# Where the modulation weights land while two projections run: slots of their own in the second branch projection and the output projection

## The chip, the cores and the metric

The kernel runs on one core of a Trainium2 chip. The core has five engines that run side by side, each through its own list of instructions in order: TensorE (PE in the profile; its weight loads stand apart as PEld) multiplies matrices, VectorE (DVE) and ScalarE (ACT) work on tiles element by element, GpSimd (POOL) and SyncE (SP) here mostly issue transfers. They meet only through semaphores. The metric is the device time in microseconds (us), the median over runs; lower is better.

## The reference

One decoder layer over 512 tokens of width 2048, in float32. A conditioning vector c is turned into six vectors of 2048 numbers ("ada", the modulation), and they shift, scale and gate the two halves of the layer:

```python
mod = (c_act @ w_ada[l] + b_ada[l])[:, None, :]
sh_a, sc_a, gt_a, sh_f, sc_f, gt_f = jnp.split(mod, N_ADA, axis=-1)
h = rms_norm(x, g_attn[l]) * (1.0 + sc_a) + sh_a
# inside parallel_mixers: sparse attention o_a, dense latent attention o_b
merged = jax.nn.sigmoid(gate_a) * (o_a @ w_pa) + jax.nn.sigmoid(gate_b) * (o_b @ w_pb)
return merged @ w_o
# and in the layer
x = x + gt_a * y
h = rms_norm(x, g_ffn[l]) * (1.0 + sc_f) + sh_f
x = x + gt_f * conv_ffn(h, w_up[l], w_conv[l], b_conv[l], w_down[l])
```

`w_ada` is 2048 x 12288. Its first third (shift and scale of the first half) is needed at the very beginning. The other two thirds are sixteen blocks of 2048 x 512, 67 MB, of which nothing is needed before the output projection ends: `gt_a` multiplies its result, `sc_f` and `sh_f` come next, `gt_f` comes last of all.

## The kernel before, in words

**Matrices.** Each float32 factor is cut into a high part that the fast matmul format holds exactly and a low part, the rest. A product is three matmuls (`mm3`, lines 117 to 119): high by high, high by low, low by high. A step of a projection, in `lin_fm` and `lin_tm` alike, takes two blocks of 128 rows by 512 columns of weights, which is one 512 KB load, one ScalarE copy that makes the high part (line 105), one VectorE subtraction that makes the low part (line 106, the tile is called `wlo`; "the correction" below), and 24 matmuls of 512 columns. The two stages called `seven` (gates of the mixer, from `w_gs`, and the feed-forward's `w_ups`) save one product in eight by adding and subtracting weight blocks first (VectorE, line 929); their steps have 24 matmuls of 256 columns, with the low parts at line 114.

**Buffers.** Weights land in a ring of five buffers, `raw` (`NR` is 5, `rawq` hands them out in turn). High and low parts have three buffers each (`NH` is 3), so a correction can run at most until three steps have been made ready and not yet multiplied. Everything else lives in 81 slots of 128 x 512 numbers, handed out first in, first out by `get` and given back by `put`.

**The ada stream.** `ada_stream` (line 702) works through the sixteen late blocks in steps, 8 steps to a block, 128 in all. One step loads 256 rows of a block's 512 columns (512 KB) and adds them, times `c_act`, to the block's accumulator `acc` with two VectorE instructions (line 720 for a block's first, line 722 for the others; "the products" below). The load goes either to one buffer of the `raw` ring (one transfer, line 714) or, while `ada_in_slots[0]` is true, to two slots (two transfers of 256 KB, line 710). A finished block waits in `pend` until `flush_cols` (lines 752 to 769) sums it over the partitions with two matmuls.

**Who calls the steps.** `ticker(rate)` returns a function that every step of a stage calls once; it adds `rate` to a credit and runs one ada step for each whole credit. The stages after the first input projection are, in the order of time of the profile before:

- the attention of branch A with some gate columns in between, until about 600 us: 35 ada steps;
- the gate stage, `seven` on `w_gs`, 56 steps, to about 795 us: rate `TS`;
- the first branch projection by `w_pa`, 16 steps, mixed with the attention of branch B, to about 1025 us: rate `TP`;
- the second branch projection by `w_pb`, 16 steps in four column blocks, to about 1127 us: rate `TB`. For each column block `load_gates` brings twelve tiles (projection A's result and both gates) through GpSimd's queue, and `ev_pb` combines them on VectorE (lines 1208, 1216, 1217, and the low part at line 114);
- the output projection by `w_o`, 32 steps in four column blocks, to about 1333 us: rate `TO`. `ev_o` multiplies by the gate and adds x (lines 1249, 1250);
- then the second norm and the feed-forward.

**Order.** The functions are written as plain loops, but the order of each engine's list is made by the framework's scheduler, which runs its own estimate of time. Weight loads and their high and low parts are issued with a raised priority (`PRI`). All weight loads and all ada loads go through SyncE's one queue, in order; a transfer waits there until its buffer is free, and everything behind it waits too.

Of the kernel before, what the change touches and what calls it, by code (L numbers as in the profile page):

```python
# [31 lines left out]
def trunk_layer_kernel(  # L32
# [8 lines left out]
    U1=4,  # L41
    U2=10,
    PLAN="A0 A1|A2 A3|B0 B1 B2 B3|A4 A5 A6 A7|B4 B5 B6 B7|A8 A9 A10 A11|B8 B9 B10 B11|A12 A13 A14 A15 B12 B13 B14 B15",
    TS=0.55,
    TP=1,
    TB=1,
    TO=1,
    HG=2,
    AFT=(-1,),
    PEU=((2, 5, 8, 11, 14),) * 2 + ((),) * 6,  # L50
# [14 lines left out]
    def get(dt=F32):  # L65
        i = free.popleft()
        if cur[i] is None or cur[i].dtype != dt:
            cur[i] = pool.tile([P, T], dt, name=f"slot{i}", tag=f"slot{i}")
        held[id(cur[i])] = i
        return cur[i]  # L70

    def getr():
        return get(F32R)

    def put(*ts):
        for t in ts:
            free.append(held.pop(id(t)))
# [415 lines left out]
    def at_bank():  # L493
        cnt["at"] += 1
        return AT[cnt["at"] % 4]
# [25 lines left out]
    for tb in range(1, 4):  # L521
# [12 lines left out]
        acc = get()  # L534
# [45 lines left out]
    def head_ss(dst, src3, i):  # L580
        n, d = src3.shape[1], src3.shape[2]
        t = sq[i % 2][:, :n * d].rearrange("p (n d) -> p n d", n=n)
        A.activation(t, src3, AF.Square)
        V.tensor_reduce(dst, t, axis=AX.X, op=ALU.add)
# [54 lines left out]
    def attend_free(kinds="pto"):  # L639
        for k in kinds:  # L640
            put(*att[k])
# [52 lines left out]

    ada_blocks = [8, 9, 10, 11, 16, 17, 18, 19, 12, 13, 14, 15, 20, 21, 22, 23]
    gst = [get(), get()]
    ada_acc = [get(), get()]

    ada_in_slots = [False]

    def ada_stream():
        for n, cb in enumerate(ada_blocks):
            assert len(pend) < 2
            acc = ada_acc[n % 2]
            for kp in range(8):
                if ada_in_slots[0]:
                    ts = [get(), get()]
                    for i in range(2):
                        k = kp * 2 + i
                        SP.dma_start(ts[i], w_ada[k * P:(k + 1) * P, cb * 512:(cb + 1) * 512])  # L710
                else:
                    raw = rawq.popleft()
                    t = raw[:, 0:1024].rearrange("p (k n) -> p k n", k=2)
                    SP.dma_start(t, w_ada[kp * 2 * P:(kp + 1) * 2 * P, cb * 512:(cb + 1) * 512]
                                 .rearrange("(k p) n -> p k n", p=P))
                    ts = [t[:, 0], t[:, 1]]
                for i in range(2):
                    k = kp * 2 + i
                    if k == 0:
                        V.tensor_scalar(acc, ts[i], c_act[:, 0:1], None, op0=ALU.mult)  # L720
                    else:
                        V.scalar_tensor_tensor(acc, ts[i], c_act[:, k:k + 1], acc,  # L722
                                               op0=ALU.mult, op1=ALU.add)
                if ada_in_slots[0]:
                    put(*ts)
                else:
                    rawq.append(raw)
                yield None
            pend.append((cb, acc))
            done[0] += 1  # L730

    pend = []
# [6 lines left out]
    def ticker(rate, fb=None):  # L739
        def tick():  # L740
            credit[0] += rate
            while credit[0] >= 1.0:
                credit[0] -= 1.0
                next(stream, None)
                age[0] = age[0] + 1 if pend else 0
                if fb and age[0] > 3:
                    flush_cols(fb())
        return tick
# [109 lines left out]
    def fill(n, ticks=0):  # L858
        for _ in range(n):
            if next(gates, 0) == 0:  # L860
                break
            for _ in range(ticks):
                tick()
# [4 lines left out]
    for hd in range(9):  # L868
# [10 lines left out]
            attend_pv(*prev)  # L879
        fill(1, 2)  # L880
        prev = state
    ada_in_slots[0] = False
    fill(26, 1)
    put(*kaT)
    put(*kva)
# [17 lines left out]
    def operands(act, ts):  # L903
        return (quarter(act, 0, 0), quarter(act, KH, 0), quarter(act, KH, HT)) + tuple(sums(ts, n) for n in range(4))
# [151 lines left out]
    def reload_mq():  # L1056
        for t in h[:KH]:
            put(*t)
        mqT.extend(reload(mq_d))

    ada_in_slots[0] = True
    seven(w_gs, (31 - G0) // 2, operands(h, h_sums), ((MM[0], MM[1]), (MM[2], MM[3])), gate_out,
          tick=ticker(TS, at_bank), near_end=reload_mq)
    ada_in_slots[0] = False
    for t in h[KH:] + [x for ts in h_sums for x in ts]:
        put(*t)
    gst = [get(), get()]
# [5 lines left out]
    def up_pair(hp):  # L1073
        kn = [get() for _ in range(2)]
        vv = [get() for _ in range(2)]
        kr = get()
        kr3 = kr.rearrange("p (t a d) -> p t a d", t=4, a=2)

        def two(ts, tb):
            o = (tb % 2) * 256  # L1080
            return ts[tb // 2][:, o:o + 256].rearrange("p (n d) -> p n d", n=2)

        def ev_up(tb, b, kn=kn, vv=vv, kr3=kr3, two=two):
            b4 = b.rearrange("p (n e d) -> p n e d", n=2, e=2)
            k3 = two(kn, tb)
            A.activation(k3, b4[:, :, 0, :], AF.Copy)
            V.tensor_copy(two(vv, tb), b4[:, :, 1, :])
            ss = sm.tile([P, 2], F32, name="ss2")
            head_ss(ss, k3, tb)
            V.tensor_scalar(ss, ss, ss_kr[:, tb:tb + 1], None, op0=ALU.add)  # L1090
            r = sm.tile([P, 2], F32, name="rs2")
            rsqrt_mean(r, ss, 192, 2)
            V.tensor_tensor(k3, k3, r[:, :, None].to_broadcast([P, 2, P]), ALU.mult)
            for a in range(2):
                V.tensor_scalar(kr3[:, tb, a], krot[:, tb], r[:, a:a + 1], None, op0=ALU.mult)

        lin_tm(w_mkv_up, hp * 512, 512, kvT, 2, MM, ev_up)
        kT = [get(), get()]
        kTr = (getr(), getr())
        for a in range(2):  # L1100
            b = at_bank()
            for tb in range(4):
                PE.transpose(b[:, tb * P:(tb + 1) * P], two(kn, tb)[:, a, :], ident)
            A.activation(kT[a], b, AF.Copy, scale=gkm_col)
        b = at_bank()
        for tb in range(4):
            PE.transpose(b[:, tb * P:(tb + 1) * P], kr[:, tb * P:(tb + 1) * P], ident)
        split(*kTr, b)
        put(*kn)
        put(kr)  # L1110

        qn = [get() for _ in range(2)]
        qr = get()
        qr3 = qr.rearrange("p (t a d) -> p t a d", t=4, a=2)
        nsc_b = sm.tile([P, 4, 2], F32, name="nsc_b", bufs=3)

        def ev_qup(tb, b, qn=qn, qr3=qr3, nsc_b=nsc_b, two=two):
            b3 = b.rearrange("p (n d) -> p n d", n=2)
            q3 = two(qn, tb)
            A.activation(q3, b3[:, :, 0:P], AF.Copy)  # L1120
            V.tensor_copy(qr3[:, tb], b3[:, :, P:192])
            ss = sm.tile([P, 2], F32, name="ss2")
            t = sq[tb % 2][:, :384].rearrange("p (n d) -> p n d", n=2)
            A.activation(t[:, :, 0:P], q3, AF.Square)
            A.activation(t[:, :, P:192], qr3[:, tb], AF.Square)
            V.tensor_reduce(ss, t, axis=AX.X, op=ALU.add)
            r = sm.tile([P, 2], F32, name="rs2")
            rsqrt_mean(r, ss, 192, 2)
            V.tensor_scalar(nsc_b[:, tb], r, -(192 ** -0.5), None, op0=ALU.mult)
            rope(qr3[:, tb], 2, 64, "qm", tb)  # L1130

        lin_tm(w_mq_up, hp * 384, 384, mqT, 4, MM, ev_qup)
        qT = [get(), get()]
        qTr = (getr(), getr())
        for a in range(2):
            b = at_bank()
            for tb in range(4):
                PE.transpose(b[:, tb * P:(tb + 1) * P], two(qn, tb)[:, a, :], ident)
            A.activation(qT[a], b, AF.Copy, scale=gqm_col)
        b = at_bank()  # L1140
        for tb in range(4):
            PE.transpose(b[:, tb * P:(tb + 1) * P], qr[:, tb * P:(tb + 1) * P], ident)
        split(*qTr, b)
        put(*qn)
        put(qr)
        pairs[hp] = (qT, qTr, kT, kTr, vv, nsc_b, two)
# [25 lines left out]
    def pa_block(cb):  # L1172
        flush_cols(MM[3])
        lin_fm(w_pa, cb * 512, oa, 8, MM, ev_store(pa_d, cb * 4), tick=ticker(TP))

    up_pair(0)
    oa = reload(oa_d)
    up_pair(1)
    attend_bufs()
    for hp in range(4):  # L1180
        attend_pair(hp)
        pa_block(hp)
        if hp < 2:
            up_pair(hp + 2)
    attend_free("pt")
    for t in oa:
        put(*t)
    for t in kvT + mqT:
# [35 lines left out]
    for cb in range(4):  # L1224
        bk = half()
        flush_cols(bk[3])
        lin_fm(w_pb, cb * 512, ob, 8, bk, ev_pb(load_gates(cb)), tick=ticker(TB))
    for t in ob:
# [37 lines left out]
    for db in range(4):  # L1266
        bk = half()
        flush_cols(bk[3])
        lin_tm(w_o, db * 512, 512, mg, KD, bk, ev_o(db), tick=ticker(TO))
    while next(stream, 0) is None:  # L1270
# [188 lines left out]
```

## Time and profile before

| | |
|---|---|
| median of 3 runs | 2723.09 us (2720.21 to 2723.1) |
| the profiled execution | 2732.41 us |
| its span on the core | 2730.6 us |
| TensorE busy | 2661.8 us, 97% of the span |
| VectorE busy | 1941.3 us, 71% |
| ScalarE busy | 1153.6 us, 42% |
| bytes moved | 437.25 MB, mean 160 GB/s |
| ada loads in `raw` buffers / in slots | 71 of 512 KB / 242 of 256 KB, of which 128 in the first stage |

Busy time counts a matmul until its modelled end, so TensorE's 97% is not 97% of its peak: where matmuls follow each other at full pace their spacing is what to look at. "Granted clock" (PEclk) is the share of TensorE's clock pulses that were let through. A row of waits names the waiting instruction, then what it waited for, then the total in us, the number of waits and the longest. A row of windows gives, for each engine, the busy us and the number of instructions in brackets, then the clock, the share of time the 16 DMA engines were busy, and GB/s.

### The profile page before, as it was taken

Reading aid. Unit: us, or ns where it says so; the run is one execution under the profiler, and the core shown is the slowest. Engines: PE = TensorE matmul, PEld = TensorE weight load, DVE = VectorE, ACT = ScalarE, POOL = GpSimd, SP = SyncE. Lnnn points to the kernel's source line nnn. Section 1 sums busy time; section 2 is a strip of 40 time slices with the busy share of each in tenths; the row PEclk is TensorE's granted clock in tenths of the full one; section 3 lists DMA queues with packets and bytes.
Section 4 is the critical chain, followed back from the end, with each engine's and each line's share of the span. In section 5 each row is a group of like instructions: output and inputs, shape, how many; then the busy total and the mean of one; then the engine's idle time right before and its main releaser. Section 6 shows DMA issues by size and latency. Waiting matters only on the chain.

```text
span 2730.6 us, 40272 instructions
## 1 busy us (share of the span) xinstructions
PE 2661.8 (97%) x15616; PEld 2303.0 (84%) x15616; DVE 1941.3 (71%) x3059; ACT 1153.6 (42%) x1713; POOL 240.9 (9%) x459
## 2 busy tenths in 40 slices
PE   6999999999999999998999999999999999999999
PEld 5777687778987767776789999999999998888887
DVE  7877966699887666745678888888888873325323
ACT  4333434334344564322445555555555553223221
POOL 1001011110022232100000000000000040000000
PEclk8999999999999999999999999999999999999999
DMA  9943137666684578755423333333333384343232
GB/s 342 341 149 100 34 103 224 199 197 211 212 273 140 175 237 257 252 179 181 138 85 122 126 113 124 117 119 120 116 128 114 119 298 129 98 125 124 93 115 78
DMA packets 197572, 437.25 MB, mean 160 GB/s; under 512 B 19290, under 2 KB 60660, under 8 KB 197380
## 3 DMA queue, kind: packets, MB, share of 16 engines
q1 hardware_dynamic: 165700, 348.59, 39.7%
q0 software_dynamic: 31648, 86.08, 9.6%
q8 instruction: 122, 2.00, 0.3%
q14 instruction: 70, 0.57, 0.1%
q10 hardware_dynamic: 32, 0.01, 0.0%
HBM read 390.56 MB, written 44.04 MB: 159 GB/s over the span
## 4 chain that ended last, share of the span: by engine, by line
PE 75%; issue 10%; DMA 8%; DVE 4%; ACT 1%; POOL 1%; SPq 0%; POOLq 0%; DVEq 0%; ACTq 0%
PE bank L117 13%; PE bank L119 13%; PE bank L118 13%; PE bank L1021 10%; PE bank L1022 10%; PE bank L1023 10%; DMA raw<-in_w_ada 4%; DMA slot<-in_w_ada 2%; DVE wlo L106 1%; DVE slot L722 1%; PE bank L1159 1%; PE bank L683 1%; DMA raw<-in_w_in 0%; DVE slot L547 0%; DMA slot<-in_x 0%
## 5 line engine op out<-in xcount | busy, mean ns | idle before, releaser
L1021 PE MATMUL bank<-slot,whi 128*128 128x256 f32 x2688 | 755.1, 282 | 12.7 <-ACT slot L978 3.2
L1022 PE MATMUL bank<-slot,whi 128*128 128x256 f32 x2688 | 754.8, 282 | 0.0
L1023 PE MATMUL bank<-slot,wlo 128*128 128x256 f32 x2688 | 748.6, 281 | 1.7 <-DVE wlo L114 1.5
L118 PE MATMUL bank<-wlo,slot 128*128 128x512 f32 (+2 forms) x1472 | 578.1, 393 | 12.2 <-DVE wlo L106 12.1
L117 PE MATMUL bank<-whi,slot 128*128 128x512 f32 (+2 forms) x1472 | 571.7, 395 | 10.4 <-ACT slot L761 4.7
L119 PE MATMUL bank<-whi,slot 128*128 128x512 f32 (+2 forms) x1472 | 572.1, 392 | 0.0
L105 ACT ACTIVATE whi<-raw 128x1024 fp32r<-128x1024 f32 (+4 forms) x270 | 280.3, 1040 | 658.6 <-PE bank L119 492.6
L113 ACT ACTIVATE whi<-raw 128x1024 fp32r<-128x1024 f32 x336 | 356.5, 1061 | 428.9 <-PE bank L1022 327.3
L1021 PEld LDWEIGHTS bank<-slot,whi 128*128 128x128 f32 x2688 | 507.9, 189 | 16.3 <-ACT slot L978 3.6
L1022 PEld LDWEIGHTS bank<-slot,whi 128*128 128x128 f32 x2688 | 506.5, 188 | 0.2
L1023 PEld LDWEIGHTS bank<-slot,wlo 128*128 128x128 f32 x2688 | 503.8, 189 | 2.7 <-DVE wlo L114 2.5
L106 DVE TENSOR_TENSOR wlo<-raw,whi 128x1024 fp32r<-128x1024 f32 (+4 forms) x270 | 323.3, 1199 | 224.8 <-ACT whi L105 224.5
L114 DVE TENSOR_TENSOR wlo<-raw,whi 128x1024 fp32r<-128x1024 f32 x336 | 409.5, 1220 | 76.1 <-ACT whi L113 74.7
L118 PEld LDWEIGHTS bank<-wlo,slot 128*128 128x128 f32 x1472 | 279.8, 190 | 77.0 <-DVE wlo L106 17.0
L117 PEld LDWEIGHTS bank<-whi,slot 128*128 128x128 f32 x1472 | 279.7, 190 | 75.5 <-ACT slot L761 6.3
L119 PEld LDWEIGHTS bank<-whi,slot 128*128 128x128 f32 x1472 | 278.6, 189 | 60.6 <-issue 0.3
L929 DVE TENSOR_TENSOR raw<-raw,raw 128x1024 f32<-128x1024 f32 x192 | 234.6, 1222 | 42.5 <-DMA raw<-in_w_ups 34.9
L118 PE MATMUL bank<-slot,whi 128*128 128x512 f32 (+1 forms) x656 | 263.3, 402 | 0.0
L117 PE MATMUL bank<-slot,whi 128*128 128x512 f32 (+1 forms) x656 | 258.8, 403 | 1.0 <-ACT slot L1294 1.0
L119 PE MATMUL bank<-slot,wlo 128*128 128x512 f32 (+1 forms) x656 | 257.2, 401 | 0.0
L114 DVE TENSOR_TENSOR slot<-slot,slot 128x512 fp32r<-128x512 f32 x152 | 103.1, 688 | 183.4 <-PE bank L118 175.1
L722 DVE SCALAR_TENSOR_TENSOR slot<-raw,c_act,slot 128x512 f32<-128x512 f32 x134 | 99.9, 748 | 95.1 <-DMA raw<-in_w_ada 93.9
(288 smaller groups left out, 2581.5 us busy)
## 6 DMA issues: line engine op xcount, KB each, us to landing
raw<-in_w_ups SPq DMA_DIRECT2D x160, 512.0 KB, 3.4
slot<-in_w_ada SPq DMA_DIRECT2D x242, 256.0 KB, 5.6
raw<-in_w_down SPq DMA_DIRECT2D x88, 512.0 KB, 3.8
raw<-in_w_ada SPq DMA_DIRECT2D x71, 512.0 KB, 4.8
raw<-in_w_in SPq DMA_DIRECT2D x50, 512.0 KB, 3.6
raw<-in_w_gs SPq DMA_DIRECT2D x32, 512.0 KB, 4.6
raw<-in_w_o SPq DMA_DIRECT2D x32, 512.0 KB, 4.4
f<-slot POOLq DMA_DIRECT2D x44, 256.0 KB, 2.4
```

Of the source, the lines that this page charges most:

```text
L105: A.activation(hi, raw[:, :w], AF.Copy)
L106: V.tensor_tensor(lo, raw[:, :w], r32(hi), ALU.subtract)
L113: A.activation(dst_hi, src, AF.Copy)
L114: V.tensor_tensor(dst_lo, src, r32(dst_hi), ALU.subtract)
L117: PE.matmul(o, lh, rh, start=first, stop=False)
L118: PE.matmul(o, lh, rl, start=False, stop=False)
L119: PE.matmul(o, ll, rh, start=False, stop=last)
L722: V.scalar_tensor_tensor(acc, ts[i], c_act[:, k:k + 1], acc, op0=ALU.mult, op1=ALU.add)
L929: V.tensor_tensor(o[:, :WN], a[:, :WN], b[:, :WN], op)
L1021: PE.matmul(o, wh[:, ks], rh, start=first and k == 0, stop=False, skip_group_check=True)
L1022: PE.matmul(o, wh[:, ks], rl, start=False, stop=False, skip_group_check=True)
L1023: PE.matmul(o, wl[:, ks], rh, start=False, stop=last, skip_group_check=True)
```

## The change

Three things change. `ada_in_slots` used to be switched off after the attention of branch A and again after the gate stage, and was off for the rest. Now it stays on from the attention of branch A, is off only while the first branch projection and branch B's attention run, and is on again for the second branch projection and the output projection. The rates change: 0.36 instead of 0.55 in the gate stage, 1.25 instead of 1 in the three projections. And there are three accumulators instead of two, so that up to three blocks can be under way.

```diff
-    TS=0.55,
-    TP=1,
-    TB=1,
-    TO=1,
+    TS=0.36,
+    TP=1.25,
+    TB=1.25,
+    TO=1.25,
...
-    ada_acc = [get(), get()]
+    ada_acc = [get(), get(), get()]
...
-            assert len(pend) < 2
-            acc = ada_acc[n % 2]
+            assert len(pend) < 3
+            acc = ada_acc[n % 3]
...
         fill(1, 2)
         prev = state
-    ada_in_slots[0] = False
     fill(26, 1)
...
-    ada_in_slots[0] = True
     seven(w_gs, (31 - G0) // 2, operands(h, h_sums), ((MM[0], MM[1]), (MM[2], MM[3])), gate_out,
           tick=ticker(TS, at_bank), near_end=reload_mq)
-    ada_in_slots[0] = False
...
+    ada_in_slots[0] = False
     up_pair(0)
...
     attend_free("pt")
+    ada_in_slots[0] = True
```

With the credits counted through, the 128 steps fall like this: 35 in branch A's attention both times; 30 before and 20 after in the gate stage; 16 and 20 in the first branch projection; 16 and 20 in the second; 31 and 33 in the output projection, where the last step comes with the stage's 31st tick before and its 27th after. In `raw` buffers there were 71 steps (8 + 16 + 16 + 31) and there are 20; in slots there were 57 and there are 108.

## The prediction

> **What bounds the kernel now.** I read the page first, then the chain that ended last, then one call of windows over the stages, and inside the two stages that stood out the waits, the chain and the groups.
>
> ```profile
> span 2730.6 us, 40272 instructions
> PE 75%; issue 10%; DMA 8%; DVE 4%; ACT 1%; POOL 1%; SPq 0%; POOLq 0%; DVEq 0%; ACTq 0%
> ```
>
> TensorE carries three quarters of the chain; what an edit elsewhere can win is the time in which TensorE is kept waiting. The windows say where that is (columns: window, length, then busy us and instructions of PE, PEld, DVE, ACT, POOL, then clock, DMA share, GB/s).
>
> ```profile
> 20.00:40.00 20.00, 17.07 (x114) 16.67 (x114) 19.40 (x37) 7.07 (x12) 0.00 (x0) 0.87 1.09 357
> 520.00:617.00 97.00, 96.93 (x443) 76.84 (x442) 79.64 (x158) 37.85 (x67) 10.80 (x20) 1.00 0.59 181
> 620.00:795.00 175.00, 161.78 (x1310) 157.91 (x1311) 152.79 (x186) 71.57 (x96) 16.43 (x31) 0.99 0.69 222
> 838.00:1020.00 182.00, 180.95 (x793) 130.06 (x793) 120.97 (x327) 102.07 (x189) 47.89 (x77) 1.00 0.59 189
> 1068.00:1127.00 59.00, 58.96 (x255) 47.40 (x254) 53.27 (x77) 24.23 (x33) 11.47 (x20) 1.00 0.87 279
> 1127.00:1333.00 206.00, 190.00 (x779) 148.96 (x778) 105.78 (x137) 48.81 (x71) 13.17 (x24) 0.97 0.57 188
> 1440.00:1740.00 300.00, 300.00 (x2531) 299.90 (x2531) 262.35 (x288) 161.62 (x212) 8.67 (x16) 1.00 0.36 120
> ```
>
> Three rows are dense: branch A's last part (520 to 617), the second branch projection (1068 to 1127) and the feed-forward's `seven` (1440 to 1740). Two are not. The output projection (1127 to 1333) leaves TensorE idle for 206.00 - 190.00 = 16.0 us, and its matmuls are stretched too: the dense projection spends 58.96 / 255 = 0.2312 us on each, so 779 need 180.1 us, and 25.9 us are lost. That pace also gives 24 x 0.2312 = 5.55 us for a step. The gate stage (620 to 795) loses 13.2 us of idle time and about 1 us of clock; its twin of the same form in the feed-forward loses nothing.
>
> In the output projection the waits name the cause: VectorE waits for ada tiles, the queue's ada loads wait for corrections, and the weight loads behind them wait with them.
>
> ```profile
> DVE slot L722 <- DMA raw<-in_w_ada: 73.8, 20, 5.9
> DVE slot L720 <- DMA raw<-in_w_ada: 12.6, 3, 5.4
> PE bank L118 <- DVE wlo L106: 11.2, 9, 2.3
> PE bank L117 <- ACT slot L761: 4.7, 3, 2.7
> ```
>
> ```profile
> SPq L714 <- DVE wlo L106: 76.2, 28, 7.5
> SPq L101 <- DMA raw<-in_w_ada: 50.0, 15, 5.5
> ```
>
> ```profile
> 1158.18 1.23 DVE wlo L106
> ...
> 1159.43 5.45 DMA raw<-in_w_ada
> ...
> 1164.97 0.76 DVE slot L722
> ...
> 1166.42 1.23 DVE wlo L106
> ...
> 1167.67 4.72 DMA raw<-in_w_ada
> ```
>
> The chain turns in a circle: a correction frees a `raw` buffer, an ada load takes it, VectorE waits for that load because the two products stand ahead of the next correction in its list, and only then the next correction runs, 8.24 us after the first, where a step of TensorE's takes 5.55. Five buffers shared by two streams are two and a half steps of lead.
>
> **The change, part by part.** Prices of single instructions come from the groups of these windows (the output projection, then the second branch projection, then the gate stage):
>
> ```profile
> L722 DVE SCALAR_TENSOR_TENSOR slot<-raw,c_act,slot 128x512 f32<-128x512 f32 x55 | 41.3, 750 | 74.7 <-DMA raw<-in_w_ada 73.8
> L106 DVE TENSOR_TENSOR wlo<-raw,whi 128x1024 fp32r<-128x1024 f32 x32 | 38.8, 1219 | 12.0 <-ACT whi L105 12.0
> ```
>
> ```profile
> L1217 DVE TENSOR_TENSOR slot<-slot,slot 128x512 f32<-128x512 f32 x13 | 8.7, 682 | 0.0
> ```
>
> ```profile
> L722 DVE SCALAR_TENSOR_TENSOR slot<-slot,c_act,slot 128x512 f32<-128x512 f32 x55 | 40.9, 746 | 8.8 <-DMA slot<-in_w_ada 8.7
> L929 DVE TENSOR_TENSOR raw<-raw,raw 128x1024 f32<-128x1024 f32 x29 | 35.3, 1219 | 5.9 <-DMA raw<-in_w_gs 5.8
> ```
>
> *Slots in the output projection.* The ring now serves weights alone: the load of step k waits for the correction of step k-5, about 28 us before its use, and no correction has to wait for an ada load that it released itself. VectorE's work stays: 105.78 us, plus two steps (33 for 31) of 2 x 0.75 us, is 108.8 of 180 us. In the changed kernel's order the 33 steps lie in the first 19; the longest run of products between two corrections is eleven, 8.3 us, against 5.55 us a step, and corrections may be two steps ahead, so it is covered. Should that lead be gone, 2.7 us are exposed once. The transfers are packed too: from the issue of the second branch's last weights to that of the output projection's tenth, ten steps, SyncE issues 17.4 MB, 313 GB/s at the dense pace, beside GpSimd's. The opening row, mostly slot tiles of 256 KB, moved 357 GB/s, so it fits, barely. Of 25.9 us I leave 4 and take a gain of 22; ends 26 (all) and 14 (half of it stays as late landings).
>
> *Rate 0.36 in the gate stage.* Ten steps leave: 20 products, 14.9 us of VectorE. Now its busy 152.79 us and its waits for tiles and weights, 8.7 + 5.8, are 167 us, more than TensorE's 161.8; afterwards 137.9 busy is 85% of that, and the dense twin has 262.35 / 300 = 87%. So the stage should come near its twin: of 14 us I take 11; ends 13 and 3 (if only the third of its tile waits that belongs to the moved steps, 8.7 / 3, goes).
>
> *Rate 1.25 and slots in the second branch projection.* Four steps more, 6.0 us of VectorE over its 16 x 5.55 = 89 us; VectorE is at 53.27 / 59 = 90% and goes to 97%. That fits only if the order is kind, and it is not everywhere: between the corrections of its steps 15 and 16 stand ten products, nine 512-column instructions of 0.68 us and the correction itself, 14.5 us together, against 5.55 us per step with at most two steps of lead. Two of the products read tiles whose slots come free inside the same run, 3.5 and 4.5 us of VectorE's work ahead. How long a landing takes in this stretch:
>
> ```profile
> L714 SPq DMA_DIRECT2D raw<-in_w_ada x50: 367/368/368, 968.1 to 1303.8; - x50
> ...
> DMA to landing us min/median/max: 3.7/5.0/8.8
> ```
>
> At the median 1.5 + 0.5 us show, at the longest 5.3 + 4.3. With up to 3 us from the run itself I take a cost of 4, near the median row, and keep 0 and 13 as ends. Behind the waiting product stand the correction for step 16 and, on TensorE, that step.
>
> *Rate 1.25 in the first branch projection.* Four more steps through the shared ring, 6 us of VectorE, which is busy 120.97 of 182 us; branch B's softmax stands in the same list. TensorE is idle 1 us there now. Cost 1; ends 0 and 5.
>
> *Slots for the eight steps around 600 us.* The row 520 to 617 has 0.07 us of idle time: nothing to win, TensorE's own work hides it; 0, and 2 if a slot comes late.
>
> *Queue and slots.* 51 steps go from one transfer to two, 51 more issues of at most 0.37 us, 19 us of SyncE over some 700; hidden, since its queue mostly waits (126 us in the output projection alone). If its lead were gone, a step would start 0.9 us later for 2.5 issues. The third accumulator takes one of 81 slots; if slots ran short, the price is that of the slower rival below. Both 0.
>
> Sum: -22 - 11 + 4 + 1 = -28 us. The profiled execution took 2732.4 us, of it 1.8 outside its span; it would take 2704. The median of the runs before lies 9.3 us lower, so I forecast 2723.1 - 28 = 2695 us.
>
> **A rule that speaks against it.** The output projection's clock is 0.97, 0.03 x 206 = 6.2 us of the 25.9, while its longest idle stretches are 2.3 and 2.7 us (the two rows of PE above); I count on the clock to come back with the gaps gone. The Trainium skill, "TensorE: Matmul & The Clock Gate", Part 1, has the clock halved after an idle window of about 3.4 us. By that rule these gaps are too short to be its cause, the slow stretches would stay, and the gain would be 22 - 6 = 16. The trace sides against it in part: the clock is 1.00 in every dense row after the opening and lower only where there are gaps.
>
> The same skill, "DMA: Bandwidth & Descriptors", section Bandwidth, wants transfers batched to 1 MiB or more for three quarters of the peak, and the change halves them; the opening row's 357 GB/s with 256 KB tiles says that size is no handicap here.
>
> **The rivals.** *Everything becomes dense*: both losses go but for a microsecond, the second branch keeps its density: -26 - 13 = -39, 2684 us. For it: the twin row, and a ring freed of its circle. Against: VectorE at 97%.
>
> *The clock stays*: 16 instead of 22, total -22, 2701 us.
>
> *The loss moves*: VectorE's in-order list carries the circle's waits into the second branch (+13), half of them stay in the output projection (-14), the gate stage wins 5, the first projection loses 4: -2, 2721 us. For it: the late slots named above. Against: the weights no longer depend on them.
>
> *Slower: gate tiles behind products.* In the changed kernel's order many of the twelve tiles of a column block go into slots that an ada product has just freed, on GpSimd's one queue:
>
> ```profile
> L1205 POOL DMA_DIRECT2D slot<-gate x3 | 1.9, 650 | 1.3 <-DVE slot L1217 1.3
> ```
>
> ```profile
> slot<-gate POOLq DMA_DIRECT2D x32, 256.0 KB, 5.5
> ```
>
> If a block's loads start only when its combination needs them, 12 x 0.65 + 5.5 = 13.3 us are exposed for each of four blocks, 53 us in place of the 4 that I took: -33 + 1 + 53 = +21, 2744 us. It decides from 8 us a block. Against: the order gives only the first two blocks such neighbours, and the loads then have 5 to 15 us of VectorE's work ahead of their use.
>
> **How the numbers follow.** My sum 0.48, the clock stays 0.14, all dense 0.18, the loss moves 0.12, slower 0.08. A difference under 0.2% (5.4 us) is no more than the measurement can tell. Of "the loss moves" I give 0.05 to faster, 0.05 to the same and 0.02 to slower. So faster 0.85, same 0.05, slower 0.10. The range goes from 2682, two below all dense, to 2717, which leaves out the slower rival and two thirds of the loss that moves.
>
> **What would show it.** In the windows after: the output projection near 184 us with clock 0.99 or more, with `DVE <- DMA in_w_ada` waits under 20 us where 86 stand now; the chain there turned to PE lines; the gate stage's PE idle time under 4 us; the second branch projection longer by about 4 us with a wait of the matmuls on `wlo` near its end. Wrong would make it: weights landing late in the first ten steps of the output projection at a DMA share near 1, a gate stage that keeps its gaps with less VectorE work, or ScalarE's sigmoids waiting for gate tiles.

## The result, and the profile after

The changed kernel takes 2701.57 us in the median (2699.17 to 2705.71, four runs); the kernel before took 2722.86 beside it. The ratio is 0.9926, with a 95% interval of 0.9908 to 0.9943: 0.7% faster, 21 us. The profiled execution took 2702.67 us, 1.1 above its median; that of the kernel before had taken 2732.41, over 9 above its own. From trace to trace the gain is therefore 29.7 us, from median to median 21.3, and the difference matters below.

The windows over the changed kernel's stages (columns as in the prediction's windows): the gate stage, the first branch projection with branch B's attention, the second branch projection, the output projection.

```profile
610.00:790.00 180.00, 168.64 (x1357) 164.40 (x1356) 152.44 (x187) 76.03 (x102) 16.27 (x31) 0.98 0.58 190
790.00:1068.00 278.00, 275.14 (x1238) 205.09 (x1237) 196.74 (x535) 150.92 (x283) 78.31 (x126) 1.00 0.67 218
1068.00:1126.00 58.00, 57.22 (x247) 45.97 (x246) 55.94 (x83) 22.40 (x32) 10.30 (x19) 1.00 0.89 305
1126.00:1305.00 179.00, 179.00 (x772) 144.54 (x771) 105.68 (x137) 49.75 (x71) 15.96 (x28) 1.00 0.61 212
```

The last row is the gain: TensorE is busy for all of 179.00 us and its clock is 1.00. The stage's waits (waiting instruction, what it waited for, total, number, longest) have turned over as well: first VectorE's largest, then those of SyncE's queue.

```profile
DVE wlo L106 <- ACT whi L105: 71.0, 22, 5.4
```

```profile
SPq L101 <- DVE wlo L106: 118.1, 26, 6.4
SPq L710 <- DMA slot<-in_w_ada: 8.2, 24, 1.3
```

VectorE no longer waits for an ada tile anywhere in the stage (86 us before). It waits for ScalarE's high parts, which wait for TensorE: the corrections are ahead of their use again. Weight loads (L101) wait for corrections, but for some 4 us in all.

The gate stage is the weak point. Its first 27 us, and the matmuls' largest waits over the whole stage:

```profile
613.00:640.00 27.00, 20.71 (x137) 18.48 (x136) 24.88 (x40) 12.93 (x20) 1.08 (x2) 0.87 0.29 98
640.00:700.00 60.00, 58.30 (x488) 57.79 (x487) 47.81 (x54) 25.11 (x33) 3.24 (x6) 1.00 0.58 191
```

```profile
PE bank L1020 <- DVE slot L988: 4.6, 4, 1.6
PE bank L1020 <- ACT slot L113: 2.6, 1, 2.6
```

Over half of its idle time, 6.3 of 11.4 us, lies in the opening, and there the clock is 0.87.

In the table each stage is measured from its first matmul to its last, from the trace's timeline, to within half a microsecond (the two projections from the end of the gate stage to the second one's last matmul). A row's stages come from one profile, and the two profiles of the kernel before differ by up to 4 us in a stage. The medians were measured beside different runs of the kernel before, whose own medians lie between 2722.86 and 2728.10 us; the ratios given with the experiments allow for that. The rows below the first three are the experiments.

| kernel | gate stage | two projections | output projection | median |
|---|---|---|---|---|
| before, first profile | 181.5 | 331.9 | 205.7 | 2723.09 |
| before, second profile | 177.3 | 333.6 | 202.2 | 2725.12 |
| changed | 175.8 | 334.7 | 179.3 | 2701.57 |
| slots in the output projection only | 176.8 | 334.5 | 180.2 | 2704.82 |
| rates and accumulator only | 171.9 | 330.8 | 189.9 | 2702.17 |
| changed, gate rate 0.55 | 180.8 | 345.0 | 179.4 | 2719.48 |
| changed, old buffers ahead of the gate stage | 173.4 | 333.1 | 179.3 | 2696.70 |
| new rates, slots in the output projection only | 169.6 | 331.3 | 181.2 | 2695.62 |
| before, ring of six | 181.0 | 327.0 | 180.3 | 2699.41 |
| before, ring of four | 181.0 | 342.8 | 180.4 | 2729.09 |
| gate rate 0.1, slots in the output projection only | 163.8 | 337.1 | 182.4 | 2696.62 |
| the same, rate 1.25 in both projections | 164.6 | 344.7 | 182.7 | 2712.68 |
| ring of six, gate rate 0.36, slots in the output projection | 179.9 | 332.3 | 181.9 | 2705.10 |
| ring of six, gate rate 0.1, slots in the output projection | 175.4 | 336.6 | 182.5 | 2712.84 |

The feed-forward's `seven` takes 795.6 to 798.4 us in all of them but the ring of four (804.0).

### The profile page after: what moved, and what is told of

It is laid out like the page before. It is cut to its first block, busy times and chain, and to the rows that moved or that the text cites. A ratio compares the mean times of both kernels' runs of the same rounds, so it can differ in the third digit from the quotient of the medians.

```text
span 2700.9 us, 40414 instructions
## 1 busy us (share of the span) xinstructions
PE 2648.9 (98%) x15616; PEld 2298.6 (85%) x15616; DVE 1942.6 (72%) x3059; ACT 1154.9 (43%) x1711; POOL 237.1 (9%) x459
## 4 chain that ended last, share of the span: by engine, by line
PE 79%; issue 13%; DMA 4%; DVE 3%; POOL 1%; ACT 0%; SPq 0%; POOLq 0%; DVEq 0%; ACTq 0%
PE bank L117 15%; PE bank L118 14%; PE bank L119 14%; PE bank L1020 10%; PE bank L1021 10%; PE bank L1022 10%; DMA slot<-in_w_ada 2%; PE bank L1156 1%; DMA gate<-slot 1%; PE bank L683 1%; DVE slot L547 0%; DMA slot<-in_x 0%; DMA raw<-in_w_ada 0%; PE bank L1157 0%; PE bank L1154 0%
## 5 line engine op out<-in xcount | busy, mean ns | idle before, releaser
L114 DVE TENSOR_TENSOR wlo<-raw,whi 128x1024 fp32r<-128x1024 f32 x336 | 409.7, 1220 | 84.2 <-ACT whi L113 83.5
L114 DVE TENSOR_TENSOR slot<-slot,slot 128x512 fp32r<-128x512 f32 x152 | 102.4, 687 | 181.7 <-PE bank L118 175.2
L722 DVE SCALAR_TENSOR_TENSOR slot<-slot,c_act,slot 128x512 f32<-128x512 f32 x203 | 150.0, 747 | 32.6 <-DMA slot<-in_w_ada 30.9
```

The source lines that it names most:

```text
L114: V.tensor_tensor(dst_lo, src, r32(dst_hi), ALU.subtract)
L722: V.scalar_tensor_tensor(acc, ts[i], c_act[:, k:k + 1], acc, op0=ALU.mult, op1=ALU.add)
```

## The experiments

**The kernel before, once more.**

> The kernel before, unchanged, for a second profile: its first profiled execution was 9 us longer than its other runs. If that execution was ordinary, the stages come out within 2 us of the first profile (gate stage 181, output projection 205) and the 9 us belong to the profiling; if it was a long one, the second profile is near 2723 and one stage at least is shorter by several us.

It took 2725.12 us (2722.8 to 2733.68); its profiled execution took 2727.79, 4.6 less than the first.

```profile
615.00:793.00 178.00, 166.62 (x1357) 163.31 (x1356) 159.99 (x197) 74.33 (x100) 17.91 (x34) 0.99 0.70 227
...
1126.00:1329.00 203.00, 188.34 (x782) 148.85 (x781) 105.76 (x138) 49.08 (x72) 13.33 (x24) 0.97 0.57 191
```

The gate stage is 4.2 us shorter than in the first profile and the output projection 3.5, while the two projections between them are 1.7 longer: the same program varies by some 4 us in those two stages. The first profile was a long execution, and the stages that I meant to cure were long in it.

**Slots in the output projection alone.** The kernel before, with

```diff
+    ada_in_slots[0] = True
     sqt = get()
     tmp_o = [get(), get()]
```

> The kernel before with one edit: the ada tiles of the output projection alone land in slots; rates, accumulators and all other stages stay. Theory of the circle (weights and ada tiles share five buffers): the output projection becomes dense, 180 to 184 us, clock 1.00, and the time is 2699 (2694 to 2703). Rival, the new spread of the steps did it, not the buffers: the output projection stays above 200 us and the time within 5 us of 2723.

2704.82 us, ratio 0.9935 (0.9924 to 0.9946). The output projection is dense at the old rates:

```profile
1126.00:1306.00 180.00, 180.00 (x776) 145.35 (x775) 106.31 (x136) 48.77 (x70) 16.75 (x29) 1.00 0.60 209
```

So who shares the buffers is enough of a cause; the new spread isn't needed for it. By itself this edit wins 18 us, where the whole change wins 21.

**Rates and third accumulator alone, buffers as before.**

> The kernel before with the new rates and the third accumulator, the buffers as they were. Theory of the circle: the output projection keeps its stalls or grows, since 33 steps go through the shared ring in 27 ticks (205 to 215 us), the second branch projection now has them too (up to 8 us more), the gate stage wins 5: 2718 to 2735. Rival, the spread did it: 2700 to 2706.

2702.17 us, ratio 0.9923 (0.9911 to 0.9936): the expectation of the circle was wrong by almost 16 us, and the rival's was met. The gate stage and the output projection, and the queue's waits in the latter:

```profile
614.00:786.00 172.00, 163.68 (x1352) 161.18 (x1351) 145.59 (x173) 74.36 (x100) 17.21 (x33) 1.00 0.61 201
...
1117.00:1307.00 190.00, 183.68 (x777) 146.24 (x776) 111.60 (x145) 49.53 (x71) 12.85 (x23) 0.99 0.65 214
```

```profile
SPq L101 <- DVE wlo L106: 67.7, 21, 7.8
SPq L714 <- DVE slot L722: 24.7, 17, 3.9
SPq L714 <- DMA raw<-in_w_ada: 23.1, 8, 5.5
SPq L101 <- DVE slot L722: 16.5, 15, 2.4
SPq L101 <- DMA raw<-in_w_ada: 11.1, 4, 5.1
SPq L714 <- DVE wlo L106: 10.1, 11, 2.4
```

The ring serves more ada loads in a shorter time, and stalls half as much. "Five buffers are too few for two streams" can't be the reason then. The same rows of the kernel before (second profile) show another:

```profile
SPq L714 <- DVE wlo L106: 73.7, 27, 7.5
SPq L101 <- DMA raw<-in_w_ada: 45.8, 16, 4.6
SPq L101 <- DVE slot L722: 36.7, 29, 3.8
```

There nearly every ada load (L714) waits for a correction, and the weight loads (L101) wait for ada loads and products: each stream waits for the other. At rate 1 the program's loads alternate, weight, ada, weight, ada, and the ring is handed out in turn. (That is the order of the program, by which the buffers are handed out; in the queue the scheduler often puts two of a kind in a row.) With five buffers a load reuses the buffer of five loads earlier, and five is odd: a weight always follows an ada tile, an ada tile always a weight. At 1.25 two ada loads follow each other once in nine loads, and then five of the nine reuse a buffer of their own kind. If so, an even ring should cure the stage, even a smaller one.

**A ring of six, and a ring of four.** The kernel before, with

```diff
-    NR, NH = 5, 3
+    NR, NH = 6, 3
...
-    n_slots=81,
+    n_slots=79,
```

> The kernel before with a ring of six buffers and 79 slots, nothing else. At a rate of 1 loads alternate, weight, ada, weight, ada; with five buffers every ada load takes the buffer that a weight tile held five loads earlier and every weight load one that an ada tile held; with six each stream reuses its own three. Theory of parity: the output projection becomes dense, 180 to 185 us. Theory of number (too few buffers): half a step more lead, 190 to 200 us.

and with `NR` of 4 and 81 slots:

> The kernel before with a ring of four buffers, 81 slots, nothing else; other stages may suffer from it, so the output projection is what is compared. Theory of parity: each stream keeps two buffers of its own, no load waits for the other stream, 180 to 190 us. Theory of number: less lead than with five, 210 us or more.

Output projection and queue, first with six, then with four buffers:

```profile
1122.00:1302.00 180.00, 180.00 (x775) 145.34 (x774) 99.77 (x126) 48.16 (x68) 12.83 (x23) 1.00 0.60 199
```

```profile
SPq L101 <- DVE wlo L106: 116.9, 32, 6.7
SPq L714 <- DVE slot L722: 27.4, 21, 3.8
SPq L714 <- DMA raw<-in_w_ada: 4.7, 4, 1.8
SPq L101 <- DVE slot L722: 2.9, 3, 1.6
SPq L101 <- DMA raw<-in_w_ada: 2.4, 1, 2.4
```

```profile
800.00:1143.00 343.00, 332.10 (x1469) 249.67 (x1468) 242.34 (x599) 174.50 (x316) 92.60 (x149) 1.00 0.66 216
1143.00:1324.00 181.00, 181.00 (x781) 146.10 (x780) 102.67 (x130) 49.75 (x73) 13.36 (x24) 1.00 0.62 204
```

```profile
SPq L101 <- DVE wlo L106: 105.0, 33, 6.8
SPq L714 <- DVE slot L722: 33.1, 22, 3.3
...
SPq L101 <- DVE slot L722: 3.2, 2, 1.6
...
SPq L101 <- DMA raw<-in_w_ada: 1.0, 2, 0.7
```

Parity holds. With four buffers, fewer than before, the output projection loses nothing. The waits of one stream for the other add up to 156 us with five buffers at rate 1 (73.7 + 45.8 + 36.7), 38 at 1.25 (16.5 + 11.1 + 10.1), 5 with six (2.9 + 2.4) and 4 with four (3.2 + 1.0); the stage takes 202, 190, 180 and 180 us. The ring of six as a whole took 2699.41 us, ratio 0.9915 (0.9898 to 0.9931), about the whole change's gain from one more buffer (and two slots fewer). Its two projections are dense too: TensorE is busy for all of the 327.0 us, where the second profile of the kernel before took 333.6. The ring of four took 2729.09 in its single run: its first row shows 10.9 us idle in the two projections, and the feed-forward is 6 us longer, so it is too small elsewhere.

**The changed kernel with the old rate in the gate stage** (`TS=0.55`).

> The changed kernel with 0.55 in the gate stage again: 30 steps there and 23 in the output projection. If the ten steps are what the gate stage won, it takes 5 us longer (180 to 182 where the changed kernel has 175.8), the output projection stays dense: 2707 (2704 to 2711). If its stalls come from its opening alone, 2700 to 2703.

2719.48 us, ratio to the kernel before 0.9988 (0.9980 to 0.9997): 18 us slower than the changed kernel, where 5 were expected. The gate stage gives 5.0 of them (180.8 against 175.8). 10.3 more lie in the two projections, at the end of the second one, the first of these two windows:

```profile
1068.00:1140.00 72.00, 66.03 (x274) 52.41 (x273) 67.68 (x101) 27.31 (x37) 14.19 (x25) 0.95 0.82 271
1140.00:1320.00 180.00, 180.00 (x776) 145.38 (x775) 90.72 (x115) 49.15 (x70) 16.77 (x30) 1.00 0.56 192
```

```profile
PE bank L758 <- DVE slot L114: 3.5, 1, 3.5
PE bank L117 <- DVE slot L765: 2.0, 1, 2.0
PE bank L757 <- ACT slot L113: 0.5, 1, 0.5
```

```profile
1118.65 0.61 DVE slot L114
1119.28 4.09 DMA slot<-in_w_ada
...
1123.80 0.75 DVE slot L722
1124.54 0.60 DVE slot L114
1125.14 1.39 DVE slot L722 x3
1126.54 0.51 issue
1127.05 0.69 DVE slot L765
1127.79 0.79 PE bank L117
```

The first two fences are the windows and the matmuls' waits, the third is the chain. The flush of a finished ada block (the matmuls of L757 and L758 in the numbering after) stands in TensorE's list; its low part (L114) stands behind ada products in VectorE's list, and one of these waits 4.09 us for its tile. TensorE waits for the flush, and the clock of that window is 0.95. The product that waits is the first one of the next block (L720), so the block had just been completed. By the credits this fits: 105 steps are done at the end of the second projection, and 104 make thirteen blocks. The rate in the gate stage sets at which step a block is complete, and so what stands ahead of a flush 300 us later.

**The changed kernel with the old buffers ahead of the gate stage.**

```diff
+    ada_in_slots[0] = False
     fill(26, 1)
+    ada_in_slots[0] = True
```

> The changed kernel, but the eight ada steps just ahead of the gate stage use the raw ring again, as before. If tiles in slots there delay the sums that open the gate stage (the run with the new rates and the old buffers has a gate stage of 172.0 us, the changed kernel 175.8), the gate stage takes 171 to 173 us and the time is 2697 (2694 to 2700). If the 3.8 us are only the luck of an order, 2699 to 2704.

2696.7 us (2695.64 to 2698.86), ratio 0.9898 (0.9884 to 0.9913), in the medians 5 us under the changed kernel. The opening and the whole of the gate stage:

```profile
613.00:640.00 27.00, 24.98 (x195) 23.89 (x194) 26.07 (x37) 14.71 (x22) 1.62 (x3) 1.00 0.50 172
```

```profile
615.00:788.00 173.00, 164.12 (x1349) 162.01 (x1348) 144.72 (x172) 73.74 (x99) 17.10 (x32) 0.99 0.61 201
```

With slots in those eight steps TensorE had 20.71 us in the opening and a clock of 0.87, without them 24.98 and 1.00. In the same 27 us VectorE ran 12 low parts of the opening sums (L114, 128x512) with the slots and 9 without: three more of them come late. Part of this is made up: in the next 60 us (640 to 700) TensorE had 58.30 us with the slots and 56.06 without, and the whole stage differs by 2.4 us (175.8 against 173.4). Why the slots put them off, whether for want of free slots or by the order alone, I didn't settle.

**New rates, slots in the output projection only.** The kernel of "rates and accumulator only" with the one added line shown above.

> New rates, third accumulator, and slots in the output projection alone: the second branch projection and the eight steps ahead of the gate stage stay in the raw ring. If slots matter only in the output projection, the gate stage is 172, the output projection dense, and the time 2693 (2689 to 2697). If the second branch projection needs its slots at the new rate, it is longer by 4 to 10 us there and the time 2698 to 2706.

2695.62 us (2692.02 to 2699.67), ratio 0.9894 (0.9878 to 0.9910). The gate stage takes 169.6 us, the output projection 181.2, and the two projections 331.3, less than the 334.7 with slots in the second one. The slots in the second branch projection bring nothing (the version before this one, which has them, took 333.1). This version and the one before it beat the kernel before by more than the intervals. Against the changed kernel (0.9926, 0.9908 to 0.9943) they are some 0.3% lower, but the intervals still overlap a little, so that this gain is likely and not shown.

**How far the gate stage goes.** The same with `TS=0.1, TP=1, TB=1, TO=2`:

> Ring of five, slots in the output projection alone, three accumulators; rates 0.1, 1, 1 and 2: five or six steps in the gate stage, some 56 in the output projection. If VectorE's ada products are what stretches the gate stage, it goes on shrinking: 177 at 30 steps, 172 at 20, so 165 to 168 here, and the output projection, with VectorE near 140 of 180 us, stays dense: 2690 (2686 to 2695). If the rest of its stalls is its opening sums, the gate stage stays at 170 to 173 and the time at 2695 to 2700.

2696.62 us, ratio 0.9900 (0.9886 to 0.9915).

```profile
614.00:778.00 164.00, 160.93 (x1349) 159.94 (x1349) 124.93 (x136) 73.47 (x98) 17.59 (x33) 1.00 0.50 164
778.00:1115.00 337.00, 331.46 (x1465) 248.31 (x1465) 240.40 (x593) 163.79 (x307) 87.03 (x139) 0.99 0.66 217
1115.00:1298.00 183.00, 183.00 (x795) 147.81 (x795) 143.80 (x199) 52.12 (x76) 17.76 (x31) 1.00 0.78 277
```

The gate stage does go on shrinking, to 163.8 us with 3.1 idle, and the output projection stays dense with VectorE at 144 of 183 us. But the two projections give 6 us back (337.1 for 331.3), and nothing is left over. To take that back I set `TP` and `TB` to 1.25 again and `TO` to 1.75:

> Ring of five, slots in the output projection alone, three accumulators, rates 0.1, 1.25, 1.25 and 1.75. With rates 0.1, 1, 1, 2 the gate stage took 163.8 us, the two projections behind it 337.1, where the run with 0.36, 1.25, 1.25 took 332.1 for them. If the longer projections come of the rate 1 in the ring of five, the gate stage keeps its 164, the projections 332, and the time is 2690 (2686 to 2694). If the steps taken out of the gate stage always cost their gain elsewhere, 2695 to 2700.

2712.68 us. The gate stage kept its 164.6, but the two projections took 344.7 and another 5.8 us passed before the output projection's first matmul. Between 1100 and 1140 us the matmuls waited there for the flush and for a weight:

```profile
PE bank L117 <- ACT whi L105: 3.2, 1, 3.2
PE bank L757 <- ACT slot L113: 2.2, 1, 2.2
```

Both expectations missed; it is the place where the old gate rate had lost its 10 us. By the credits, 80 steps are done at the end of the second projection, which is ten blocks exactly, so again a block is completed just there. That this alone makes the loss wasn't tried.

**Ring of six with the new gate rate.** The ring has six buffers, with 79 slots, slots for the ada tiles of the output projection and three accumulators; the rates are 0.36, 1, 1 and 1.5, then 0.1, 1, 1 and 2.

> Ring of six with 79 slots, slots in the output projection alone, three accumulators, rates 0.36, 1, 1 and 1.5. The gains of the ring (26 against the kernel before, of which the output projection is 22 and the rest elsewhere) and of the gate rate (5) add up: 2692 (2687 to 2697). If two slots fewer hold up the gate stage (it was 181 us with six buffers at the old rate), 2697 to 2703.

> The same with rates 0.1, 1, 1 and 2. If both add up, 2687 (2682 to 2692); if two slots fewer hold up the gate stage, 2692 to 2700.

2705.1 us and 2712.84 us: the gains don't add up. The output projection is dense in both (181.9 and 182.5). The gate stage is not: it takes 179.9 us in the first, where the ring of six took 181.0 at the old rate. The matmuls' largest waits there, in the first of these two kernels and then in the ring of six at the old rate:

```profile
PE bank L1021 <- ACT slot L113: 6.6, 2, 6.3
```

```profile
PE bank L1021 <- DVE slot L989: 7.5, 5, 4.8
```

With six buffers the stage has stalls of its own at either rate; the second kernel here has the first one's again (6.6, longest 6.2), and its gate stage takes 175.4 us where the ring of five at the same rate took 163.8. That isn't the whole loss. Beside the ring of six at the old rates, profile against profile, the first kernel also reaches its gate stage 7.8 us later and takes 5 us more in the two projections (its profiled execution was 5.6 us above its median); the second wins 5.6 us in the gate stage and gives back 9.6 in the two projections (336.6 for 327.0). Both times miss even the loss that I had allowed for. Whether the slots given up for the sixth buffer are the reason, I didn't try.

## Why the prediction was right

I forecast 2695 us, with 2682 to 2717 around it; 2701.57 lies inside, and the sign and most of the size came from the stage that was named. Step by step:

*Output projection: -22 forecast, ends 26 and 14.* Measured -26.4 against the first profile, -22.9 against the second. What was to show it came: 179 us, clock 1.00, no wait of VectorE for ada tiles, a chain of TensorE rows. That loads of the two streams wait for each other was the right cause. The sentence that gave the reason, "five buffers shared by two streams are two and a half steps of lead", was wrong: four buffers give less lead and the stage is as dense. The odd number was the reason. My price for the slots was near all the same, because slots take the ada stream out of the ring altogether, and that cures the stage under either reason.

*Clock.* It came back with the gaps gone, 0.97 to 1.00, in the changed kernel, with slots alone and with both even rings: the rival in which it stays falls. It fell to 0.87 in the 27 us of the changed kernel's gate-stage opening, where no wait of the matmuls was longer than 2.6 us; in that stretch it was 0.50 from 625.0 to 631.7 us, about the end of that wait and behind it. In the first profile of the kernel before it was 0.50 from 1294.4 to 1297.7 us, behind a wait of 2.66 us that ended at 1293.3. The Trainium skill, "TensorE: Matmul & The Clock Gate", Part 1, lets it drop after an idle window of about 3.4 us. The measurement decides: here a lower clock goes with shorter gaps than that.

*Gate stage: -11 forecast, ends 13 and 3.* This step failed: -5.7 against the first profile, inside the ends, and -1.5 against the second, outside them. A sign of being wrong that I had named came with it: the stage keeps most of its gaps with less VectorE work. From its first to its last matmul VectorE is busy 147.2 us where it was 158.6 in the first profile, but TensorE is still idle 9.5 us, where I had wanted under 4 (14.1 and 11.4 in the two profiles before). It contains two terms that I sized wrongly. The rate is worth 7 us, not 11: with the old buffers ahead of the stage it takes 181.5, 177.3 and 176.8 us at 0.55 (mean 178.5), and 171.9, 173.4 and 169.6 at 0.36 (mean 171.6). These are single profiles, and those of one rate differ by up to 4.7 us, so the 7 is rough; with slots ahead of the stage the rate gives 5.0 (180.8 and 175.8). And the slots in the eight steps ahead of it, "0, and 2 if a slot comes late", cost 2.4 to 4: 175.8 for the 173.4 of the run that takes them back, or for the mean of 171.6. The row 520 to 617, on which I rested the 0, was dense and stayed so; the price fell due in the opening of the next stage.

*Two projections: +5 forecast (pb +4, pa +1).* Measured +2.8 against the first profile, +1.1 against the second; the second branch projection itself is dense but for 0.8 us. I had the sign, over-priced it and had the place wrong: the matmuls wait 0.8 us in the second branch projection, for a flush (L765) and not for `wlo` as I had named, and 2.7 us in the first one. The end of 13 isn't far-fetched: with the gate rate at 0.55 the same place lost 10 us, by the flush and not by the correction for step 16 that I had named.

*Queue and third accumulator: 0.* Nothing shows against it in the changed kernel; neither was tried by itself.

*The sum.* From profile to profile it is -29.7 for a forecast of -28, from median to median -21.3. I took the sum off the median, though the execution that it was read from was 9.3 us longer than that median. The second profile of the kernel before says where: its gate stage is 4.2 us shorter and its output projection 3.5. So the sum promised to win some 8 us that an ordinary execution hadn't lost. That -29.7 came so near to -28 is partly luck: 4 us too few for the output projection and 2 too many for the two projections make up for 5 too many that I had hoped for in the gate stage.

*The rivals.* "Everything becomes dense" is half right, for the output projection alone. "The loss moves" didn't happen in this kernel and did in its relative with the old gate rate. The slower one, gate tiles late on GpSimd's queue, didn't come: the second branch projection lost 0.8 us in all.

## What to carry to other kernels

When two streams take turns in one ring of buffers, write down which load's buffer each load inherits: with an odd ring and strict alternation every load inherits a buffer of the other stream, and in this kernel's output projection one buffer more, or even one fewer, removed the stall. A stall whose cause is a shared resource can be lifted in several ways that don't add up (in the medians: slots in the output projection -18, new rates -21, both together -30, the ring of six -26, all of the change -21; the ring with new rates and slots only -19), so each part wants its own run before it is kept. Take the loss of a stage from an execution that stands near the median, or from two, before it enters a sum against the median.

## What I had not expected of the hardware

The same program's stages vary from one execution to the next, and not all alike: in the two profiles of the kernel before the gate stage took 181.5 and 177.3 us and the output projection 205.7 and 202.2, where a stage without stalls repeated within 0.3 us (the feed-forward's `seven`, 798.2 and 797.9). The program's first three runs, within 2.9 us of each other, hadn't suggested it; in 23 later ones it took 2715.38 to 2728.11 us. In these two profiles it is the stalled stages that vary; two are few.
